# Decoded sequences: values as the left operand in plain fp32, 32 weight columns per pair of heads

## The chip, the cores and the metric

The kernel runs on one core of a Trainium2 chip. The metric is the device time of one execution in microseconds (us); a version is timed in several runs. PE is TensorE (PEld its weight loads), DVE is VectorE, ACT is ScalarE, POOL is GpSimd, and SP is the engine that issues most DMAs.

## What is computed

One layer of a streaming encoder on 512 prompt frames (one sequence) and 8 decoded sequences of 16 frames each (`DEC_BATCH` 8, `DEC_SEQ` 16), that is 640 tokens of width 2048, all in float32. One input projection feeds two groups of heads, whose outputs are normed, joined, projected, and followed by a SwiGLU of width 5632:

```python
def sample_layer(x, ck_a, cv_a, ck_b, cv_b, w_in, norm_mix, rel_table, sinks, ...):
    qa, ka, va, qb, kb, vb = split_proj(rmsnorm(x, norm_mix) @ w_in)
    qb, kb = rope_partial(qb, pos), rope_partial(kb, pos)
    oa = band_attend(qa, concat([ck_a, ka]), concat([cv_a, va]), ..., bias=bias)   # 16 heads of 64
    ob = band_attend(qb, concat([ck_b, kb]), concat([cv_b, vb]), ..., sink=sinks)  # 16 q heads, 2 kv heads
    return merge_and_ffn(x, oa, ob, ...), ka, va, kb, vb

def band_attend(q, k, v, valid, bias=None, sink=None):
    s = einsum('bgqhrd,bgkhd->bghrqk', q, k) * HEAD_DIM ** -0.5        # + bias
    p = exp(s - m)                                                     # m = max (with the sink)
    w = p / (sum(p) + exp(sink - m))                                   # the sink in group B only
    return einsum('bghrqk,bgkhd->bgqhrd', w, v)
```

A decoded sequence of group A has 256 cached keys per head and 16 own ones; one of group B has 128 cached keys and 16 own ones.

## The kernel before

**Split operands.** A matmul operand is mostly held as two fp32r tiles, a rounded part and a rest: `split` writes `hi` on ACT (L179) and `lo = src - hi` on DVE (L180), and `mm3` makes a product of three matmuls (L188 to L190). A matmul whose operands are plain fp32 tiles is given to TensorE as it stands; the transposes (`tr`, L303) and the norms' sums (L232) and spreads (L244) are of that kind. In the trace each of the 42 matmuls of L232 is two records with two weight loads (84 in all); a transpose is one.

**Order of the work.** PE's stream is a row of dense products (`dense`: a chunk of 8 blocks of 128 rows by two halves of 320 tokens by three matmuls; tiles `dn`). After each block `tick` adds `n.rate` to a counter and lets `pump` advance a side job to its next `yield`. Side jobs stand in two queues: `heads` (attention of the prompt, one pair of heads a job) and `decode` (`decode_b`, `decode_a(0)`, then `decode_a(1)`); with two streams they take turns. They come in after four of the eight pairs are projected, with a rate of 1.1. After the last projection `drain_queue("decode")` runs what is left of `decode_a(0)` without ticks between, and advances `heads` jobs in turn with it; then `group_operands` loads the eight tiles of group B's output (`ob_d`), scales and splits them (L183 on ACT, L184 on DVE) and sums their squares (L261 on ACT, L262 on POOL); then comes the output projection of group B (`w_out_b`, 16 blocks `m`), whose ticks pump `decode_a(1)`. At `m == 11` four tiles of `oa_d` are loaded in the same way. The order that the program builds is then changed by a list scheduler, engine by engine, under its own estimates; `keep_pace` holds a side matmul behind the last dense one ahead of it.

**One sequence of `decode_a`.** A job handles a group `g` of 8 heads (four pairs `t` of two heads). For each of the 8 sequences it scatters the 16 queries of each head into zeroed tiles `z` (L633, DVE), loads the cached keys (`cka`), splits them, and makes the scores of all 8 heads at once, 128 rows (8 heads by 16 queries) by 272 keys, in 12 matmuls (4 pairs of 3). Softmax: L656 (bias, maximum), L657, the exponentials with their sums L658 and L659 on ACT, L665 and L666 on DVE (sum, reciprocal). The weights `pt` (unscaled, 128 by 384: 256 cached keys, and 128 columns in which only the sequence's own 16 are not zero) are turned round by `flip`: three transposes and a split. Each half of the cached values (`cva`, 128 keys by 512 columns of 8 heads) is split, and multiplied with the weights as left operand, 512 columns moving: three matmuls per half, and three more with the own values `vh`. The result has 128 rows by 512 columns, of which a head needs its own 64 columns; L684 scales it by `den` (DVE, 128 by 512), four transposes turn it, and two copies (L693) take from it the diagonal blocks.

**One sequence of `decode_b`.** For each of two halves of four sequences it loads keys, values and queries into `S` tiles and splits all of them into pairs of `D` tiles; the own keys are copied from `kb` by POOL. Per sequence: scores in two products of 64 rows by 144 columns (L571), softmax (L574 to L584; here the weights are scaled before they are turned), four transposes, a split, and two products of 256 columns (L592, L593).

**Tiles.** SBUF tiles are drawn from lists (`S`: 128 by 640; `W`: 128 by 1024; `D`: six to ten tiles handed over from other lists); a tile that is drawn again waits for the last use of its former owner.

Of the kernel before, what the change touches and what calls it, by code (L numbers as in the profile page):

```python
# [8 lines left out]
ALU = mybir.AluOpType  # L9
# [265 lines left out]
def diagonal(ap, first):  # L275

    return bass.AP(tensor=ap.tensor, offset=ap.offset + first, ap=[list(ap.ap[0]), [160, 4], [1, DS]])


def r(ap):  # L280
    return ap.bitcast(F32R)


def build(nc, tc, io, pools):
# [32 lines left out]
    sa_d, sb_d = dram("sa_d", (3, P, 8, P)), dram("sb_d", (P, 8, P))  # L317

# [6 lines left out]
    kb = (r(kb0), r(kb1))  # L325
    vb_own = tuple(r(x[:, SP:]) for x in (vb0, vb1))
# [82 lines left out]
    def flip(blocks, lst):  # L409
# [10 lines left out]
        return own, hl  # L420

# [121 lines left out]
    def decode_b():  # L543
        os_b = n.get("W")
        o_s = sh(os_b, 8, P)
        for hf in range(2):
            kraw, vraw, qraw = n.get("S"), n.get("S"), n.get("S")
            dma(out=sh(kraw, 4, CB), in_=io["ckb"][:, 4 * hf:4 * hf + 4])
            dma(out=sh(vraw, 4, P), in_=io["cvb"][:, 4 * hf:4 * hf + 4])
            dma(out=sh(qraw, 8, 64), in_=sb_d[:, :, 64 * hf:64 * hf + 64])  # L550
            yield
            qo, ko, vo = [(n.get("D"), n.get("D")) for _ in range(3)]
            qd = [r(sh(x, 4, 8, DS)) for x in qo]
            n.split(sh(qraw, 8, 64).rearrange("p t (b s) -> p b t s", b=4), *qd)
            kd = [r(sh(x, 4, CB + DS)) for x in ko]
            n.split(sh(kraw, 4, CB), kd[0][:, :, :CB], kd[1][:, :, :CB])
            for e in range(2):
                src = f(kb[e])[:, SP + 64 * hf:SP + 64 * hf + 64].rearrange("p (b s) -> p b s", b=4)
                nc.gpsimd.tensor_copy(kd[e][:, :, CB:], src)
            vd = [r(sh(x, 4, P)) for x in vo]  # L560
            n.split(sh(vraw, 4, P), *vd)
            n.put("S", kraw, vraw, qraw)
            yield
            for bb in range(4):
                b = 4 * hf + bb
                pts = []
                for j in range(2):
                    rows = slice(64 * j, 64 * j + 64)
                    ps = n.bank()[:, :CB + DS]
                    qq = [qd[e][rows, bb].rearrange("p t s -> p (t s)") for e in range(2)]  # L570
                    n.mm3(ps, qq, (kd[0][rows, bb], kd[1][rows, bb]), True, True)  # L571
# [16 lines left out]
                own, pt2 = flip([pts[0][1][:, :P], pts[1][1][:, :P], pts[0][1][:, P:], pts[1][1][:, P:]], "S")  # L588
# [16 lines left out]
    def decode_a(g):  # L605
# [5 lines left out]
        for i in range(3):  # L611
# [6 lines left out]
            else:  # L618
                ps = n.bank().rearrange("p (a b) -> p a b", a=4)
                for j in range(4):  # L620
                    tr(ps[:, j], sv[:, j])
# [5 lines left out]
        for b in range(NB):  # L627
# [60 lines left out]
            for t in range(4):  # L688
                tr(pf[:, P * t:P * t + P], od[:, P * t:P * t + P])
# [527 lines left out]
```

## Time and profile before

| what | us |
|---|---|
| median of 3 runs (lowest, highest) | 2656.42 (2656.01, 2658.73) |
| the profiled execution | 2658.85 |
| its span, first to last instruction | 2657.1 |
| mean granted TensorE clock | 0.992 |

The decoded sequences take part from about 440 us (first scores of `decode_b`: 456 us) to about 830 us (last transpose of the side jobs: 826 us) of the span; the last projection ends at about 664 us, the first product of `w_out_b` begins there. A line of a group gives line, engine, operation, tiles written and read, shape, count, then busy time, mean duration of one in ns, and the engine's idle time ahead of them with what ended it. [...]

### The profile page before, as it was taken

The page shows a single profiled execution, that of the slowest core. Times are in us where ns is not written, and L with a number is a line of the kernel's source. Part 1 is how long each engine was busy: PE and PEld are TensorE (multiplying, and loading weights), DVE is VectorE, ACT ScalarE, POOL GpSimd, SP SyncE. Part 2 cuts the span into 40 slices and gives each one's busy share as a digit, 9 for nine tenths or more (in the row PEclk, how much of TensorE's full clock was granted, in tenths as well). Part 3 has the DMA queues.
Part 4 walks back from the last instruction along what each step waited for, and adds up shares of the span by engine and source line. Part 5 has one row for each costly group of instructions (what it writes and reads, how often), then busy time and mean ns, then how long its engine had stood idle before and what let it go on. Part 6 is the DMA issues. An engine that isn't in the chain of part 4 may idle for free.

```text
span 2657.1 us, 44937 instructions
## 1 busy us (share of the span) xinstructions
PE 2590.4 (97%) x17565; PEld 2532.0 (95%) x17565; DVE 1894.7 (71%) x2934; ACT 1112.5 (42%) x1830; POOL 765.4 (29%) x584
## 2 busy tenths in 40 slices
PE   8999999999999999999999999999999899999996
PEld 8999998999899999999999999999999899999996
DVE  5665566655866877676676677667667988878797
ACT  5443344444633543333333333333334444455553
POOL 0000000000211223433433433343345533444463
PEclk9999999999999999999999999999999899999998
DMA  5322232433655433333333333333335744467665
GB/s 169 106 72 80 90 103 87 129 119 128 221 179 182 155 118 101 118 105 103 123 99 112 119 105 105 114 105 108 119 103 167 222 135 126 134 152 179 154 154 154
DMA packets 162549, 342.58 MB, mean 129 GB/s; under 512 B 19072, under 2 KB 77440, under 8 KB 162336
## 3 DMA queue, kind: packets, MB, share of 16 engines
q1 hardware_dynamic: 151824, 326.92, 38.9%
q0 software_dynamic: 9360, 11.47, 2.7%
q8 instruction: 138, 2.26, 0.4%
q10 hardware_dynamic: 1152, 1.31, 0.1%
q14 instruction: 75, 0.61, 0.1%
HBM read 284.70 MB, written 54.20 MB: 128 GB/s over the span
## 4 chain that ended last, share of the span: by engine, by line
PE 70%; DVE 6%; DMA 3%; issue 2%; ACT 2%; SPq 0%; POOL 0%; DVEq 0%; ACTq 0%; POOLq 0%
PE dn L188 14%; PE dn L190 14%; PE dn L189 14%; PE at L188 9%; PE at L189 9%; PE at L190 9%; DVE W L180 2%; PE at L303 1%; DMA S<-act_d 1%; DVE S L924 1%; DMA W<-w_down 1%; DVE S L180 1%; DMA S<-cka 1%; ACT W L179 1%; DVE S L941 0%
## 5 line engine op out<-in xcount | busy, mean ns | idle before, releaser
L188 PE MATMUL dn<-S,W 128*128 128x320 f32 x3694 | 1161.4, 314 | 11.8 <-DVE S L924 5.5
L190 PE MATMUL dn<-S,W 128*128 128x320 f32 x3694 | 1148.6, 311 | 14.5 <-DVE W L180 14.3
L189 PE MATMUL dn<-S,W 128*128 128x320 f32 x3694 | 1146.6, 310 | 2.0 <-DVE S L180 1.1
L179 ACT ACTIVATE W<-W 128x1024 fp32r<-128x1024 f32 (+2 forms) x632 | 608.2, 963 | 1024.6 <-PE dn L189 538.5
L180 DVE TENSOR_TENSOR W<-W,W 128x1024 fp32r<-128x1024 f32 (+2 forms) x632 | 761.1, 1204 | 157.8 <-ACT W L179 152.6
L188 PEld LDWEIGHTS dn<-S,W 128*128 128x128 f32 x3694 | 697.3, 189 | 24.5 <-issue 9.2
L190 PEld LDWEIGHTS dn<-S,W 128*128 128x128 f32 x3694 | 696.9, 189 | 20.5 <-DVE W L180 19.1
L189 PEld LDWEIGHTS dn<-S,W 128*128 128x128 f32 x3694 | 697.4, 189 | 4.6 <-DVE S L180 1.3
L190 PE MATMUL at<-S,W 128*128 128x320 f32 x1594 | 494.6, 310 | 4.2 <-DVE W L180 4.1
L188 PE MATMUL at<-S,W 128*128 128x320 f32 x1594 | 493.5, 310 | 0.0
L189 PE MATMUL at<-S,W 128*128 128x320 f32 x1594 | 493.3, 309 | 0.0
L907 POOL TENSOR_TENSOR W<-W,W 128x1024 f32<-128x1024 f32 (+2 forms) x76 | 163.4, 2150 | 583.1 <-DVE W L180 502.0
L190 PEld LDWEIGHTS at<-S,W 128*128 128x128 f32 x1594 | 299.8, 188 | 7.7 <-DVE W L180 7.4
L189 PEld LDWEIGHTS at<-S,W 128*128 128x128 f32 x1594 | 300.1, 188 | 0.0
L188 PEld LDWEIGHTS at<-S,W 128*128 128x128 f32 x1594 | 300.0, 188 | 0.0
L924 DVE TENSOR_TENSOR S<-S,dn 128x320 f32<-128x320 f32 x358 | 164.2, 481 | 100.6 <-PE dn L190 99.4
L903 DVE TENSOR_TENSOR W<-W,W 128x1024 f32<-128x1024 f32 (+2 forms) x76 | 135.6, 1784 | 102.9 <-DMA W<-w_up 50.7
L914 POOL TENSOR_TENSOR W<-W,W 128x1024 f32<-128x1024 f32 (+2 forms) x76 | 165.4, 2177 | 105.9 <-DVE W L180 102.8
L924 DVE TENSOR_TENSOR S<-S,at 128x320 f32<-128x320 f32 x262 | 123.3, 480 | 71.2 <-PE at L190 71.2
L262 POOL TENSOR_TENSOR S<-S,S 128x640 f32<-128x640 f32 x40 | 74.6, 1865 | 156.6 <-ACT S L261 153.4
L905 DVE TENSOR_TENSOR W<-W,W 128x1024 f32<-128x1024 f32 (+2 forms) x76 | 82.8, 1090 | 33.4 <-DMA W<-w_gate 25.8
L517 POOL MEMSET S<- 80x640 f32 x9 | 6.3, 695 | 330.0 <-DMA ob_d<-S 212.2
(153 smaller groups left out, 2269.2 us busy)
## 6 DMA issues: line engine op xcount, KB each, us to landing
W<-w_gate SPq DMA_DIRECT2D x88, 512.0 KB
W<-w_up SPq DMA_DIRECT2D x88, 512.0 KB
W<-w_in SPq DMA_DIRECT2D x66, 512.0 KB
W<-w_down SPq DMA_DIRECT2D x64, 384.0 KB
W<-w_down SPq DMA_DIRECT2D x68, 320.0 KB
act_d<-S SPq DMA_DIRECT2D x63, 320.0 KB
half<-act_d SPq DMA_DIRECT2D x81, 160.0 KB
S<-act_d SPq DMA_DIRECT2D x80, 160.0 KB
```

The costliest lines, as they stand in the source:

```text
L179: self.nc.scalar.activation(hi, src, AF.Identity)
L180: self.nc.vector.tensor_tensor(lo, src, f(hi), ALU.subtract)
L188: mm(out, a[0], b[0], start=first, stop=False)
L189: mm(out, a[0], b[1], start=False, stop=False)
L190: mm(out, a[1], b[0], start=False, stop=last)
L262: (eng or nc.gpsimd).tensor_tensor(ssq, ssq, sq, ALU.add)
L303: nc.tensor.transpose(out, src, n.ident)
L903: nc.vector.tensor_tensor(b12[:, w], b12[:, w], b22[:, w], sub)
L905: nc.vector.tensor_tensor(s6[:, w], b11[:, w], b12[:, w], sub)
L907: nc.gpsimd.tensor_tensor(b11[:, w], b22[:, w], s6[:, w], sub)
L914: nc.gpsimd.tensor_tensor(b21[:, w], b21[:, w], s6[:, w], sub)
L924: add = lambda o, a, b: nc.vector.tensor_tensor(o, a, b, ALU.add)
```

## The change

Group A's weights are now scaled in place by `den` (one DVE operation of 128 by 384, ahead of the turn), turned by three transposes and copied once by ACT as plain fp32 (`flip_whole`). Cached values stay as they were loaded, and the own ones are copied once as plain fp32 (`v_own`). The product is turned round: for each pair `t` the 128 value columns of its two heads are the left operand and 32 columns of weights (two heads by 16 queries) move, for two cached halves and the own block: 12 plain fp32 matmuls, which give the output in the layout that is needed; L684, the four transposes and the strided `diagonal` are gone. A sequence of `decode_a` has 10 `yield`s now, and had 14. In group B queries, keys, values and weights are plain fp32: one matmul per product in place of three; the own keys and values take a way through a DRAM tile `kv_d`, and all loads go straight into `D` tiles.

```diff
+    def flip_whole(blocks, lst):
+        w = P * len(blocks)
+        ps = n.bank()[:, :w]
+        for i, src in enumerate(blocks):
+            tr(ps[:, P * i:P * i + P], src)
+        own = n.get(lst)
+        nc.scalar.activation(own[:, :w], ps, AF.Identity)
+        return own
...
     def decode_b():
...
-            kraw, vraw, qraw = n.get("S"), n.get("S"), n.get("S")
-            dma(out=sh(kraw, 4, CB), in_=io["ckb"][:, 4 * hf:4 * hf + 4])
...
+            ko, vo, qraw, qo = (n.get("D") for _ in range(4))
+            kd, vd, qd = sh(ko, 4, CB + DS), sh(vo, 4, P), sh(qo, 4, P)
+            dma(out=kd[:, :, :CB], in_=io["ckb"][:, 4 * hf:4 * hf + 4])
+            dma(out=kd[:, :, CB:], in_=kv_d[0, :, 64 * hf:64 * hf + 64].rearrange("p (b s) -> p b s", b=4))
...
-                    n.mm3(ps, qq, (kd[0][rows, bb], kd[1][rows, bb]), True, True)
+                    nc.tensor.matmul(ps, qd[rows, bb], kd[rows, bb], start=True, stop=True)
...
-                n.mm3(po, (vd[0][:, bb], vd[1][:, bb]), cut(pt2, 0, 256), True, False)
-                n.mm3(po, vb_own, cut(pt2, 256, 512), False, True)
+                nc.tensor.matmul(po, vd[:, bb], own[:, :256], start=True, stop=False)
+                nc.tensor.matmul(po, v_own[:, :P], own[:, 256:512], start=False, stop=True)
...
     def decode_a(g):
...
             nc.vector.reciprocal(den, den)
+            nc.vector.tensor_scalar(pt[:, :CA + P], pt[:, :CA + P], den, None, ALU.mult)
             yield
             yield
-            own3, p3 = flip([pt[:, P * j:P * j + P] for j in range(3)], "S")
+            own3 = flip_whole([pt[:, P * j:P * j + P] for j in range(3)], "S")
             n.put("S", pt)
             yield
+            yield
             po = n.bank()
-            for j in range(2):
-                two, vd = pair("S", 512)
-                n.split(raws[j][:, :512], *vd)
-                n.put("S", raws[j])
-                yield
-                yield
-                n.mm3(po, cut(p3, P * j, P * j + P), vd, j == 0, False)
-                n.put("S", *two)
-            n.mm3(po, cut(p3, 256, 384), [x.rearrange("p a b -> p (a b)") for x in vh], False, True)
-            n.put("S", *own3)
-            od = n.get("S")
-            nc.vector.tensor_scalar(od[:, :512], po, den, None, ALU.mult)
-            yield
-            yield
-            pf = n.bank()
+            keys = (*raws, v_own)
             for t in range(4):
-                tr(pf[:, P * t:P * t + P], od[:, P * t:P * t + P])
-            n.put("S", od)
+                for j, v in enumerate(keys):
+                    nc.tensor.matmul(po[:, 32 * t:32 * t + 32], v[:, P * t:P * t + P],
+                                     own3[:, P * j + 32 * t:P * j + 32 * t + 32],
+                                     start=t == j == 0, stop=(t, j) == (3, 2))
+            n.put("S", own3, *raws)
...
-                nc.vector.tensor_copy(sh(o_s, 4, P)[rows, :, own], diagonal(pf[rows], DS * rr))
+                nc.vector.tensor_copy(sh(o_s, 4, P)[rows, :, own],
+                                      sh(po, 4, 32)[rows, :, DS * rr:DS * rr + DS])
+            yield
```

In the rows below, a name is a tile with its number of the build; `dn` are dense products, `at` the banks of the side jobs, and lines move down by up to 9 in the changed file (transposes L303 become L298, scores of the prompt L379 become L374). Rows follow each other on the engine.

PE, in `w_out_b`, from the turn of a sequence's weights (`decode_a(1)`, its third sequence here) to the product with the values, before:

```order
L303 MATMUL at_8244<-cst,S_1466_8207 128x128 x3
L190 MATMUL dn_8231<-S_1364_7775,W_1474_8234 128x320
L188 MATMUL dn_8231<-S_1368_7784,W_1473_8233 128x320
L189 MATMUL dn_8231<-S_1369_7785,W_1473_8233 128x320
L190 MATMUL dn_8231<-S_1368_7784,W_1474_8234 128x320
L188 MATMUL dn_8231<-S_1368_7784,W_1473_8233 128x320
L189 MATMUL dn_8231<-S_1369_7785,W_1473_8233 128x320
L190 MATMUL dn_8231<-S_1368_7784,W_1474_8234 128x320
L188 MATMUL at_8258<-S_1479_8259,S_1476_8248 128x512
```

and after (the second sequence):

```order
L298 MATMUL at_8106<-cst,S_1397_8087 128x128 x3
L188 MATMUL dn_8033<-S_1273_7489,W_1389_8035 128x320
L189 MATMUL dn_8033<-S_1274_7490,W_1389_8035 128x320
L190 MATMUL dn_8033<-S_1273_7489,W_1390_8036 128x320
L188 MATMUL dn_8033<-S_1273_7489,W_1389_8035 128x320
L675 MATMUL at_8124<-S_1401_8110,S_1398_8093 128x32
L675 MATMUL at_8124<-S_1401_8110,S_1399_8094 128x32
L675 MATMUL at_8124<-S_1401_8110,S_1309_7602 128x32
```

Between the turn and the product stand four dense matmuls now. This is so in 7 of the 16 sequences; in 3 more there are six or eight, in the others 19 rows and more. Between the last scores and the turn there stand at least 18 dense matmuls or other side work as long; before, 11 or 12 in half of the sequences.

DVE, one sequence of `decode_a(1)` from its maximum (L656, then L653) to the copies of its output, before:

```order
L656 ISA S_1501_8394,sm_8391<-at_8329,S_1398_7860 128x272
L656 ISA sm_8391 128x1
L633 CAST S_1400_7862<-S_1403_7868 64x4x16 x2
L657 TENSOR_SCALAR sm_8391<-sm_8391 128x1
L180 TENSOR_TENSOR S_1548_8636<-S_1534_8571,S_1547_8635 128x512
L665 TENSOR_TENSOR sm_8392<-sm_8392,sm_8393 128x1
L666 RECIPROCAL sm_8392<-sm_8392 128x1
L180 TENSOR_TENSOR S_1507_8418<-at_8413,S_1506_8417 128x384
L797 TENSOR_TENSOR S_1514_8452<-dn_8342,S_1358_7764 128x640
```

and after:

```order
L653 ISA S_1419_8224,sm_8221<-at_8159,S_1289_7533 128x272
L653 ISA sm_8221 128x1
L630 CAST S_1291_7535<-S_1294_7541 64x4x16 x2
L654 TENSOR_SCALAR sm_8221<-sm_8221 128x1
L662 TENSOR_TENSOR sm_8222<-sm_8222,sm_8223 128x1
L663 RECIPROCAL sm_8222<-sm_8222 128x1
L664 TENSOR_SCALAR S_1420_8225<-S_1420_8225,sm_8222 128x384
L681 COPY S_1288_7532<-at_8262 64x4x16 x2
```

The turn now comes after L662, L663 and L664, ahead of which it stood before; the splits of the values and of the turned weights (L180) and the scaling of the result (L684, further down) are gone.

PE, at the end of the last projection (`dn_7302` before, `dn_7274` after are its bank; `dn_7840` and `dn_7509` are the first of `w_out_b`), before:

```order
L190 MATMUL dn_7302<-S_72_213,W_1272_7415 128x320
L188 MATMUL dn_7840<-S_1361_7768,W_1395_7842 128x320
L303 MATMUL at_7526<-cst,S_1290_7521 128x128 x4
L188 MATMUL at_7491<-S_1288_7511,S_1283_7481 128x512
L189 MATMUL at_7491<-S_1289_7512,S_1283_7481 128x512
```

and after:

```order
L190 MATMUL dn_7274<-S_72_214,W_1242_7366 128x320
L188 MATMUL dn_7509<-S_1250_7437,W_1284_7511 128x320
L189 MATMUL dn_7509<-S_1251_7438,W_1284_7511 128x320
L190 MATMUL dn_7509<-S_1250_7437,W_1285_7512 128x320
L188 MATMUL dn_7509<-S_1250_7437,W_1284_7511 128x320
L189 MATMUL dn_7509<-S_1251_7438,W_1284_7511 128x320
```

Before, `decode_a(0)` still had its sequences 6 (in part) and 7 to do at this point, and the attention of the last pair of prompt heads ran between too. With fewer `yield`s `decode_a(0)` ends within the last projection, 84 dense matmuls ahead of its end: `w_out_b` runs on in a row, and the last pair of heads is pumped within it, in turn with `decode_a(1)`.

More of the change, by code (lines that the diff above doesn't have):

```diff
@@ L708, in build @@
     dma(out=io["o_kb"], in_=kf)
-    n.split(kf, *kb)
+    n.split(kf[:, :SP], *kb)
+    dma(out=kv_d[0], in_=kf[:, SP:])
     n.put("F", kf)
@@ L715, in build @@
     tr(ps, vf[:, SP:])
-    n.split(ps, *vb_own)
+    vs = n.scratch()[:, :P]
+    nc.scalar.activation(vs, ps, AF.Identity)
+    dma(out=kv_d[1], in_=vs)
     n.put("F", vf)
```

55 lines of the change are left out of this document (22 added, 33 removed).

## The prediction

> **What bounds the kernel now.** First the page: engine totals and the chain that ended last.
>
> ```profile
> span 2657.1 us, 44937 instructions
> PE 2590.4 (97%) x17565; PEld 2532.0 (95%) x17565; DVE 1894.7 (71%) x2934; ACT 1112.5 (42%) x1830; POOL 765.4 (29%) x584
> PE 70%; DVE 6%; DMA 3%; issue 2%; ACT 2%; SPq 0%; POOL 0%; DVEq 0%; ACTq 0%; POOLq 0%
> ```
>
> PE is busy for 97% of the span and makes 70% of the chain. DVE and ACT time alone is worth nothing; the change counts by what PE has to do and by how long PE waits. Second, the stretches with decoded work (columns: length, then busy us of PE, PEld, DVE, ACT and POOL with counts, clock, DMA share, GB/s), and one of the FFN beside them:
>
> ```profile
> 440.00:655.00 215.00, 211.65 (x1433) 197.04 (x1433) 135.55 (x356) 93.54 (x211) 12.97 (x53) 1.00 0.39 122
> 655.00:705.00 50.00, 46.54 (x305) 40.85 (x304) 41.95 (x103) 36.85 (x78) 15.95 (x21) 1.00 0.63 201
> 705.00:830.00 125.00, 120.35 (x781) 114.39 (x780) 79.83 (x159) 42.47 (x81) 14.53 (x32) 0.99 0.58 190
> 440.00:840.00 400.00, 388.55 (x2582) 362.27 (x2582) 265.79 (x623) 180.38 (x377) 48.73 (x109) 1.00 0.48 157
> 1000.00:2045.00 1045.00, 1045.00 (x7129) 1045.00 (x7129) 723.32 (x767) 365.54 (x396) 397.57 (x217) 1.00 0.34 111
> ```
>
> From 440 to 840 us PE is idle for 400 - 388.55 = 11.45 us. That is the size of what fewer waits can bring there, beside some 0.16 us more at each wait (a 320 column matmul lasts 0.31 us but the next starts after 0.147), which the busy column hides. DVE is busy for 66% and ACT for 45%: neither is the bound.
>
> **Prices on PE**, from start to start. The timeline of PE around a value product of group A, around four transposes, and around six plain fp32 matmuls (12 records):
>
> ```profile
> 648.25 0.39 PE L188 MATMUL at<-S,S 128*128 128x512 f32 x1
> ...
> 649.64 0.30 PE L188 MATMUL dn<-S,W 128*128 128x320 f32 x1
> 110.24 0.60 PE L303 MATMUL at<-cst,S 128*128 128x128 f32 x4
> 110.59 0.39 PE L188 MATMUL dn<-S,W 128*128 128x320 f32 x1
> 110.83 0.31 PE L189 MATMUL dn<-S,W 128*128 128x320 f32 x1
> 696.20 1.39 PE L232 MATMUL at<-cst,S 128*128 128x1 f32 x12
> 697.45 0.39 PE L188 MATMUL dn<-S,W 128*128 128x320 f32 x1
> 697.68 0.31 PE L189 MATMUL dn<-S,W 128*128 128x320 f32 x1
> ```
>
> Six matmuls of 512 columns: 1.39 us, 0.231 each. Four transposes: 110.83 - 110.24 less one dense matmul (0.147) = 0.44, 0.110 each. Twelve fp32 records with one column: 697.68 - 696.20 - 0.147 = 1.33, 0.111 each. With one column to move, that is the loading of 128 columns of weights; a plain fp32 matmul is two such records, 0.222 us.
>
> **Group A on PE.** Per sequence and job, 16 times: nine matmuls of 512 columns (9 x 0.231 = 2.08) and four transposes (0.44) go; twelve fp32 matmuls come, 24 records x 0.111 = 2.66, since 32 columns are nearer to L232's one than to anything that fills the load. So +0.14 each, **+2.3 us**. A way past the load isn't to be seen: every record has other weights.
>
> **Group B on PE.** Per sequence:
>
> ```profile
> 456.04 0.31 PE L190 MATMUL dn<-S,W 128*128 128x320 f32 x1
> 456.27 0.34 PE L188 MATMUL at<-S,S 64*128 64x144 f32 x2
> ...
> 457.02 0.31 PE L189 MATMUL dn<-S,W 128*128 128x320 f32 x1
> 484.68 0.28 PE L188 MATMUL at<-S,S 128*128 128x256 f32 x1
> ...
> 485.40 0.31 PE L188 MATMUL dn<-S,W 128*128 128x320 f32 x1
> ```
>
> The scores: six matmuls take 457.02 - 456.04 - 2 x 0.147 = 0.69. Four fp32 records come. If each streams as an fp32r one does, the load sets 0.111 each (0.44); if each needs two steps a column, 288 steps, which is next to a dense matmul of 320 (0.147; 0.13 by proportion) gives 0.53. The values: six of 256 columns take 0.72; four records come, at 0.12 each (0.48) by the first reading, or at the 0.231 of 512 columns (0.92) by the second. No row has a plain fp32 matmul with more than 128 columns, so both ends stand: -0.25 to -0.16 and -0.24 to +0.20, times 8. I take the slow end, -1.3 and +1.6, **+0.3 us**, since two records for one matmul say that the operands are cut up, and keep -3.9 as the other end.
>
> [...] The 84 records of 42 matmuls speak for two loads.
>
> **Waits on the turned weights (group A).** Groups of PE's transposes and of the operations at issue, and the timeline of one turn:
>
> ```profile
> L303 PE MATMUL at<-cst,S 128*128 128x128 f32 x461 | 76.4, 278 | 10.0 <-ACT S L658 5.8 <-DVE S L583 1.6 <-DVE S L684 1.2
> L407 DVE TENSOR_SCALAR S<-S,sm 128x384 f32<-128x384 f32 x16 | 6.6, 414 | 0.0
> L684 DVE TENSOR_SCALAR S<-at,sm 128x512 f32<-128x512 f32 x16 | 11.9, 746 | 7.9 <-PE at L190 7.1 <-POOL S L645 0.7
> 657.86 0.29 PE L190 MATMUL at<-S,S 128*128 128x272 f32 x1
> 659.46 0.51 ACT L658 ACTIVATE S<-S,sm 128x256 f32<-128x256 f32 x1 [3.91 <-DVE sm L657]
> 660.12 0.62 PE L303 MATMUL at<-cst,S 128*128 128x128 f32 x3 [0.35 <-ACT S L658]
> 660.58 0.16 DVE L666 RECIPROCAL sm<-sm 128x1 f32<-128x1 f32 x1
> 660.77 0.49 ACT L179 ACTIVATE S<-at 128x384 fp32r<-128x384 f32 x1 [0.42 <-PE at L303]
> ```
>
> The turn waits 5.8 us in all for the exponentials, in 8 places, 7.1 with the hidden 0.16 each. Now it starts 2.26 us after the last score matmul (657.86 to 660.12). With the scaling ahead of it, it can start at 660.74 + 0.41 and a hand-over, some 661.2: 3.3 us. The order gives 18 to 20 dense matmuls as cover in 6 places (18.5 x 0.147 = 2.7, with the mode's 0.1 some 2.85), so 0.45 us each, 2.7; in the others the cover is longer. A DVE split of 0.69 that happens to stand ahead in half of them adds about 3. So 5.7 in place of 7.1, **-1.4 us** (from -7, all covered, to +7, a delay at each of 16).
>
> The four transposes that waited for L684 (1.2 us on PE, three waits, 1.7 with the hidden part) go: **-1.7**.
>
> **A new wait: the product on ACT's copy.** In the rows above the copied weights are ready at 661.26, 1.14 us after the first transpose started. In 7 places the product stands behind three transposes and four dense matmuls, 0.33 + 0.59 + 0.1 = 1.0: 0.15 us each, 1.1 in all, and where a weight split (1.06 us on ACT) stands ahead of the copy, up to that more. I take one such, **+2**; from 0 to 10 x 1.06. Behind the waiting matmul stands all dense work, so it is paid in full.
>
> **The end of the projections.** Before, 40 us of side work with hardly any dense matmuls lie there, and the loading of group B's output beside it. PE's waits:
>
> ```profile
> 664.56 0.41 PE L188 MATMUL dn<-S,W 128*128 128x320 f32 x1 [0.34 <-ACT S L183]
> 679.24 0.42 PE L189 MATMUL dn<-S,W 128*128 128x320 f32 x1 [0.96 <-DVE S L184]
> 691.66 0.39 PE L196 MATMUL at<-S,W 128*128 128x256 f32 x1 [0.61 <-DVE S L180]
> 692.52 0.41 PE L303 MATMUL at<-cst,S 128*128 128x128 f32 x2 [0.32 <-DMA S<-sa_d]
> L183 ACT ACTIVATE S<-S,cst 128x640 fp32r<-128x640 f32 x8 | 6.6, 824 | 3.4 <-DMA S<-ob_d 3.4
> L261 ACT ACTIVATE S<-S 128x640 f32<-128x640 f32 x7 | 5.1, 731 | 0.0
> ```
>
> The stretch 655 to 705 has 50 - 46.54 = 3.46 us idle, 4.4 with six hidden parts. After, the eight tiles can be made beside 84 dense matmuls (12.3 us): ACT needs 8 x (0.82 + 0.73) = 12.4, and the first tile is ahead of them. So nearly all of it goes: **-4** (from 0, if tiles in slots that the projection still reads come late, to -6).
>
> **At no cost.** DVE loses per sequence two value splits, the turned weights' split and L684 and gains the scaling, about 2.3 us, 36 in all; ACT two splits of the values. PE's dense work was ready anyway (FFN row: PE never idle at a DVE share of 69%). SP gets five DMAs more (`kv_d`), issued under projections; a late one would cost PE a DMA's landing, as here:
>
> ```profile
> 687.95 4.43 DMA S<-sa_d
> ```
>
> The second half's queries now go into a tile that the first half's last product reads; until its scores there are 36 matmuls, some 5 us, against 4.4 and ACT's copy. I book 0, at worst +1.
>
> **Sum.** +2.3 + 0.3 - 1.4 - 1.7 + 2 - 4 = -2.5 us. The profiled execution, 2658.85, would come to 2656.4; the median of the runs shown is 2.4 below it, so the forecast is **2654 us** (2656.42 - 2.5), within the 0.2% (5.3 us) that a measurement of this kernel can tell from no change.
>
> **Rivals.**
> - Faster. The relief of DVE and ACT takes three quarters of the 11.45 us of idle time (8.6), and group B streams at the fast end (-3.9 with A's +2.3): 2656.4 - 8.6 - 1.6 = 2646. For it: nearly all waits are on DVE or ACT. Against: the longest chain, scores to turn, gets longer. Chance 0.27.
> - Slower: the copy on ACT. If a weight split stands ahead of it at the ten places with up to eight dense matmuls between, PE loses 10 x 1.06 = 10.6; with +2.6 of PE work and -4: 2666. It decides from some 0.8 us a place. For it: ACT takes its work in order, and some copies stand right behind such a split. Against: ACT is 45% busy. Chance 0.13.
> - [...] Chance 0.02.
> - The forecast, waits of another kind for the same time: 0.58.
>
> **Range.** 2646 to 2664: from the faster rival to just under the slower. Faster by over 0.2%: 0.27; within: 0.58; slower: 0.15.
>
> **What the profile after should show.** L675: 384 records (16 x 24) with 0.111 us from start to start; group B's product at 0.12 or 0.23. No idle time of PE on L183 or L184 ahead of `w_out_b`, and its bank following the projection's at once. L298 waiting for DVE L664 rather than for ACT, some 6 us in all; L675 waiting for L423, 1 to 3 us. PE's idle time from 440 to 840 near 8 us. I am wrong if L675 waits for over 0.5 us at a place, if its records take more than 0.12, or if the load of values (`cva`) becomes what L675 waits for: before, ACT's splits waited for it.

## The result, and the profile after

The changed kernel takes 2678.93 us (median of 4 runs, 2674.09 to 2681.80) against 2656.22 (4 runs, 2655.69 to 2658.73): slower, ratio 1.0082, 95% interval 1.0063 to 1.0100. The profiled execution has a span of 2674.7 us, 17.6 more than before.

The page's engine totals, and the stretches that were read before (length, busy us of PE, PEld, DVE, ACT and POOL with counts, granted clock, DMA share, GB/s):

```profile
span 2674.7 us, 45112 instructions
PE 2605.4 (97%) x17709; PEld 2553.8 (95%) x17709; DVE 1847.0 (69%) x2869; ACT 1092.0 (41%) x1794; POOL 769.4 (29%) x580
440.00:655.00 215.00, 209.17 (x1416) 195.18 (x1415) 113.03 (x329) 80.98 (x193) 15.85 (x51) 0.97 0.37 115
655.00:705.00 50.00, 46.21 (x322) 43.69 (x321) 35.50 (x66) 29.03 (x54) 17.87 (x18) 0.97 0.61 197
705.00:830.00 125.00, 118.75 (x795) 115.53 (x794) 66.20 (x153) 40.43 (x84) 15.00 (x34) 0.92 0.56 179
440.00:840.00 400.00, 384.13 (x2602) 364.40 (x2601) 218.69 (x552) 152.96 (x333) 48.72 (x102) 0.95 0.46 146
```

DVE and ACT have less to do, as forecast, and PE 144 records more (17709 against 17565). What the sum had not at all is the third column from the right: the granted clock, 1.00 from 440 to 840 us before, is 0.95 now and 0.92 from 705 to 830. PE's idle time is 15.87 us there (400 - 384.13), 4.4 more than before.

The trace's clock is at one of two values, full and half (1.00 and 0.50). In the decoded part it is at half in five stretches now (37.5 us in all) and was in one before (3.4 us, at 800.6). Around one of them, timeline rows of all engines, and the stretches ahead of it, in it and in the longest one:

```profile
735.31 0.31 PE L190 MATMUL dn<-S,W 128*128 128x320 f32 x1
736.05 0.42 DVE L664 TENSOR_SCALAR S<-S,sm 128x384 f32<-128x384 f32 x1
736.62 0.52 PE L298 MATMUL at<-cst,S 128*128 128x128 f32 x3 [1.00 <-DVE S L664]
737.17 0.49 ACT L423 ACTIVATE S<-at 128x384 f32<-128x384 f32 x1 [1.62 <-PE at L298]
737.42 0.30 PE L188 MATMUL dn<-S,W 128*128 128x320 f32 x1
...
740.21 1.47 PE L675 MATMUL at<-S,S 128*128 128x32 f32 x6
741.49 0.61 PE L189 MATMUL dn<-S,W 128*128 128x320 f32 x1
741.90 0.47 PE L190 MATMUL dn<-S,W 128*128 128x320 f32 x1
742.17 0.47 PE L188 MATMUL dn<-S,W 128*128 128x320 f32 x1
742.43 0.47 PE L189 MATMUL dn<-S,W 128*128 128x320 f32 x1
```

```profile
735.85:739.26 3.41, 2.64 (x21) 2.42 (x21) 0.51 (x2) 0.49 (x1) 0.00 (x0) 1.00 0.92 325
739.26:746.08 6.82, 6.82 (x29) 6.82 (x29) 2.48 (x5) 2.10 (x3) 0.75 (x3) 0.50 0.35 130
810.94:824.59 13.65, 13.18 (x57) 13.21 (x58) 4.74 (x8) 2.28 (x3) 1.66 (x2) 0.50 0.17 48
```

The transposes wait 1.0 us for the scaling, four dense matmuls follow, then the product with the values. At 739.26 the clock falls. Dense matmuls then start 0.267 us apart (741.90, 742.17, 742.43) in place of 0.147, records of the product 0.213 (741.49 - 740.21 over 6) in place of 0.11. In a stretch at half clock some 45% of the time is lost: 37.5 x 0.46 = 17 us, 1.5 before. The first row of the stretches is the surprise: in the 3.41 us ahead of the fall PE was listed as busy for 2.64.

The edges of the clock in this trace lie on one grid of 3.41 us (from 739.26 to 810.94 there are 21 steps). For each step of the grid I counted how long columns were streaming. It is an estimate: columns of each matmul by 0.42 ns, twice for plain fp32, since records of L589 and L590 with 256 columns start 0.215 us apart, 0.84 ns a column, where fp32r matmuls with 512 start 0.231 apart, 0.45 ns a column. The steps ahead of the five falls, and the lowest steps at full clock that were followed by none:

```
fall at us          531.0  599.3  684.6  739.3  810.9
half clock for us     6.8    6.8    3.4    6.8   13.7
share streamed ahead 0.30   0.38   0.33   0.36   0.23
longest wait ahead   2.8    1.3    4.1    1.3    3.1   (start to start of PE)

no fall, step at    636.9  715.4  551.5  752.9  677.8
share streamed       0.37   0.38   0.39   0.39   0.43
```

By this count the threshold lies near 0.37 to 0.38, and the same count parts the steps of all 20 traces of this study. From 440 to 2600 us, 96 steps at full clock were followed by a fall, all with shares of up to 0.38; 12432 were not, all with shares of 0.365 and more. (Transposes count as plain fp32. The prompt's scores, fp32r on 64 of the 128 rows, count half each: those with 256 columns start in pairs, at 484.34 and 484.35 for one.) How busy PE is listed does not part them: 79 of the steps without a fall have PE busy for 0.6 of the time or less, and five falls, in `a_only` and `narrow_defer_sq` below, follow a step in which PE was busy throughout. Here is one such step of each kernel, first of a_only, then of narrow_defer_sq, where L674 is the product, and PE's rows in the latter:

```profile
794.91:798.32 3.41, 3.41 (x29) 3.41 (x30) 0.44 (x2) 0.00 (x0) 0.00 (x0) 1.00 0.83 317
806.25:809.66 3.41, 3.41 (x29) 3.27 (x29) 0.36 (x2) 0.09 (x1) 0.00 (x0) 1.00 0.38 118
806.09 0.30 PE L189 MATMUL dn<-S,W 128*128 128x320 f32 x1
806.39 2.87 PE L674 MATMUL at<-S,S 128*128 128x32 f32 x24
809.09 0.39 PE L190 MATMUL dn<-S,W 128*128 128x320 f32 x1
```

A product of 24 records with 32 columns streams 24 x 64 x 0.42 = 0.65 us of its 2.66, 0.24; with 0.75 us of dense matmuls to fill the step without a gap, that is 0.39. So the product by itself stands at the threshold. A wait of a microsecond in the same step brought it below (1.00 us at 736.62, share 0.36); in the rows above, 0.15 us did, by which the product started late (806.39 - 806.09 - 0.147; share 0.32).

PE's waits from 440 to 840 us (total, times, longest):

```profile
PE at L298 <- DVE S L664: 8.1, 10, 2.8
PE at L298 <- DVE S L363: 4.5, 2, 3.8
PE at L298 <- ACT W L179: 2.5, 1, 2.5
PE at L675 <- ACT S L423: 0.4, 1, 0.4
```

Each run comes with its mean clock, so its time can be cut in two: what the clock took (span x (1 - clock), an upper bound, since idle time at half clock costs nothing) and the rest. The clock is given to 0.001, which is 2.7 us. Both parts are means over a kernel's runs, so they do not add up to the median exactly. All kernels of this study; each ratio is to the runs of before on the same chip, and the row of before has those of one chip (the runs of before on other chips give 16.6 to 18.6 and 2636.3 to 2638.3):

| kernel | median us | ratio to before (95%) | clock us | rest us |
|---|---|---|---|---|
| before (20 runs) | 2654.9 | | 18.3 | 2636.7 |
| after | 2678.9 | 1.0082 (1.0063 to 1.0100) | 36.1 | 2642.3 |
| a_only | 2681.7 | 1.0100 (1.0086 to 1.0114) | 36.8 | 2644.6 |
| b_only | 2653.4 | 0.9994 (0.9986 to 1.0003) | 19.8 | 2634.1 |
| w64 | 2668.2 | 1.0053 (1.0040 to 1.0066) | 29.3 | 2639.7 |
| wide | 2665.9 | 1.0043 (1.0029 to 1.0058) | 24.0 | 2642.1 |
| spread | 2665.4 | 1.0036 (1.0022 to 1.0050) | 24.5 | 2640.0 |
| late_turn | 2670.1 | 1.0061 (1.0048 to 1.0073) | 32.6 | 2638.5 |
| wide_late | 2664.0 | 1.0033 (1.0021 to 1.0044) | 24.4 | 2639.3 |
| before10 | 2660.6 | 1.0021 (1.0012 to 1.0030) | 22.7 | 2638.0 |
| wide14 | 2666.5 | 1.0042 (1.0029 to 1.0055) | 24.5 | 2641.7 |
| b18 | 2676.4 | 1.0081 (1.0068 to 1.0095) | 30.1 | 2646.5 |
| warm | 2661.6 | 1.0027 (1.0016 to 1.0039) | 18.0 | 2643.9 |
| b_warm | 2658.3 | 1.0012 (1.0003 to 1.0020) | 17.6 | 2640.6 |
| noscale | 2656.4 | 1.0005 (0.9996 to 1.0014) | 20.3 | 2636.2 |
| wide_sq | 2657.8 | 1.0009 (1.0000 to 1.0018) | 19.8 | 2638.2 |
| b_sq | 2659.3 | 1.0014 (1.0005 to 1.0024) | 22.2 | 2636.4 |
| defer | 2660.0 | 1.0022 (1.0013 to 1.0031) | 21.8 | 2638.8 |
| defer_sq | 2656.9 | 1.0007 (0.9998 to 1.0015) | 18.6 | 2638.4 |
| narrow_defer_sq | 2656.7 | 1.0011 (1.0002 to 1.0020) | 22.9 | 2634.7 |

Of the change's loss, some 17.8 us are the clock (36.1 - 18.3) and 5.6 the rest.

### The profile page after: what moved, and what is told of

The parts are those of the page before. It is cut to its first block, busy times and chain, and to the rows that moved or that the text cites. A ratio compares the mean times of both kernels' runs of the same rounds, so it can differ in the third digit from the quotient of the medians.

```text
span 2674.7 us, 45112 instructions
## 1 busy us (share of the span) xinstructions
PE 2605.4 (97%) x17709; PEld 2553.8 (95%) x17709; DVE 1847.0 (69%) x2869; ACT 1092.0 (41%) x1794; POOL 769.4 (29%) x580
## 4 chain that ended last, share of the span: by engine, by line
PE 85%; DVE 7%; DMA 3%; ACT 2%; issue 2%; SPq 0%; POOL 0%; DVEq 0%; ACTq 0%; POOLq 0%
PE dn L188 18%; PE dn L190 18%; PE dn L189 18%; PE at L190 8%; PE at L188 8%; PE at L189 8%; DVE W L180 2%; PE at L675 2%; PE at L298 2%; PE at L374 1%; DMA S<-act_d 1%; DVE S L917 1%; DMA W<-w_down 1%; ACT W L179 1%; PE at L196 1%
## 5 line engine op out<-in xcount | busy, mean ns | idle before, releaser
L180 DVE TENSOR_TENSOR W<-W,W 128x1024 fp32r<-128x1024 f32 (+2 forms) x632 | 758.3, 1200 | 160.9 <-ACT W L179 155.6
L190 PEld LDWEIGHTS dn<-S,W 128*128 128x128 f32 x3694 | 699.6, 189 | 20.0 <-DVE W L180 18.6
L262 POOL TENSOR_TENSOR S<-S,S 128x640 f32<-128x640 f32 x40 | 77.4, 1936 | 173.9 <-ACT S L261 173.1
L898 DVE TENSOR_TENSOR W<-W,W 128x1024 f32<-128x1024 f32 (+2 forms) x76 | 82.1, 1080 | 29.6 <-DMA W<-w_gate 24.4
```

What stands on the lines that cost most here:

```text
L180: self.nc.vector.tensor_tensor(lo, src, f(hi), ALU.subtract)
L190: mm(out, a[1], b[0], start=False, stop=last)
L262: (eng or nc.gpsimd).tensor_tensor(ssq, ssq, sq, ALU.add)
L898: nc.vector.tensor_tensor(s6[:, w], b11[:, w], b12[:, w], sub)
```

## The experiments

**Is it the clock, and what brings it down?** The width of the product came first. `wide` is after with this edit:

```diff
-                    nc.tensor.matmul(po[:, 32 * t:32 * t + 32], v[:, P * t:P * t + P],
-                                     own3[:, P * j + 32 * t:P * j + 32 * t + 32],
+                    nc.tensor.matmul(po[:, P * t:P * t + P], v[:, P * t:P * t + P],
+                                     own3[:, P * j:P * j + P],
...
-                                      sh(po, 4, 32)[rows, :, DS * rr:DS * rr + DS])
+                                      diagonal(po[rows], DS * rr))
```

> All 128 columns of the turned weights move through each value block in place of 32; same number of matmuls, same order on PE, and the copies take the diagonal. In the changed kernel the granted clock is 0.95 from 440 to 840 us (five stretches at half clock, 37.6 us) against 1.00 before. Theory 1, the clock falls after a stretch of 3.4 us in which few columns stream, however long the matmuls are listed as busy: 128 columns fill the time that the loading of weights takes, so L675 stays at 0.111 us from start to start, stretches at half clock remain only behind waits of some 2.8 us and more (three), 10 to 14 us in all, and the time falls by 10 to 14 us, to 2665 to 2669. Theory 2, the waits of the transposes for L664 bring the clock down and the shape of the product has no part in it: same as the changed kernel, 2676 to 2682. Theory 3, a plain fp32 record is paid by its columns: L675 rises to 0.21 us and the time to 2700 or more.

2665.9 us, 13.0 below after; the clock's part falls from 36.1 to 24.0, the rest stays (2642.3 and 2642.1). Four times the columns take no longer: the trace of wide has the product and its neighbours so, and the stretches and waits:

```profile
745.31 0.30 PE L188 MATMUL dn<-S,W 128*128 128x320 f32 x1
745.61 2.94 PE L675 MATMUL at<-S,S 128*128 128x128 f32 x24
748.31 0.39 PE L189 MATMUL dn<-S,W 128*128 128x320 f32 x1
```

```profile
440.00:655.00 215.00, 210.06 (x1464) 195.91 (x1463) 116.05 (x339) 83.77 (x200) 17.02 (x53) 1.00 0.38 120
705.00:840.00 135.00, 129.16 (x929) 125.46 (x928) 75.08 (x152) 45.24 (x84) 22.15 (x38) 1.00 0.61 195
440.00:840.00 400.00, 385.05 (x2709) 365.13 (x2708) 229.16 (x563) 160.13 (x341) 56.00 (x107) 1.00 0.49 156
```

```profile
PE at L298 <- DVE S L664: 7.7, 10, 2.3
PE at L298 <- DVE S L363: 4.9, 2, 4.2
```

24 records in 2.70 us (748.31 - 745.61), 0.112 each, as with 32 columns. The waits are the same as after's, and the clock stays up but for one stretch behind the wait of 4.2 us. So the waits alone don't bring it down, and theory 2 falls; nor are columns the price (theory 3).

`w64` moves 64 columns (two pairs of heads, of which the copies take one):

> 64 columns move in place of 32 (two pairs of heads, of which one is kept); order and matmuls as in the changed kernel. Theory 1, a threshold on the streamed share: the product's own share is 0.48 in place of 0.24, stretches with a wait of about 1 us come to 0.45 to 0.55, above the threshold, so the clock is as with 128 columns: 2664 to 2670. Rival, the loss goes down with the columns in proportion: half way between 32 and 128 columns, some 2672 to 2674.

2668.2, inside theory 1's band, though not for its reason. It had the clock as with 128 columns, but the clock's part, 29.3, lies between those of 32 and 128: in the profiled execution it falls three times from 440 to 840 (676, 731, 806 us; shares of 0.17, 0.37 and 0.38 ahead), so 64 columns still leave two steps at the threshold.

`spread` puts `if t: yield` ahead of each pair's three matmuls:

> One more yield between the pairs of heads, so that the 24 records of a product fall into four pieces of six with dense matmuls between. Theory 1 (few streamed columns in 3.4 us): each stretch of 3.4 us holds some 0.7 to 1.4 us of the product at most, so half clock only behind the long waits, 10 to 14 us in all: 2663 to 2670. Thirteen yields in place of ten also move the end of group A's first half later, up to 4 us the other way. Theory 2 (the waits alone): same as the changed kernel, 2676 to 2682, clock near 0.95 from 440 to 840.

2665.4. The same cure by another way: the records are as narrow as after's, but stand in pieces of six between dense matmuls, and the clock's part is wide's (24.5 and 24.0).

`late_turn` moves the last `yield` of a sequence to behind L664, and `wide_late` does so in wide:

> The changed kernel with one of group A's ten yields moved from the end of a sequence to between the scaling L664 and the transposes, so that the transposes wait less; 32 columns as in the changed kernel. Theory 1 (half clock after 3.4 us in which columns stream for less than some 0.37 of the time): the product alone with the dense matmuls around it gives 0.38 to 0.39, so with short waits it stays above, and half clock is left only behind the two or three waits of 2.8 us and more: 2663 to 2670, clock from 440 to 840 near 0.98 to 0.99. Rival, the 32 columns bring the clock down whatever the transposes wait for: 2674 to 2682.

> 128 columns and the moved yield together. From wide's 2666: of its 7.7 us of waits for L664 some 5 go, and what remains above the kernel before is group A's price on PE (2.3 us) and the waits at the end of the projections: 2658 to 2663. If the waits come back in another place, or the moved yield makes other work late: 2664 to 2668.

2670.1 and 2664.0. In late_turn nine steps with the narrow product stay at full clock with shares of 0.38 to 0.41; the clock falls only behind three waits of about 3 us. That is 8.8 us less than after, 3.5 of them the clock's part, just above theory 1's band (the clock from 440 to 840 us is 0.97, below what it said); with the same yields 128 columns are 6 us better still. Wide_late lies 1 us above its first band: the waits for L664 hardly fell (7.5 us in 8 places), and the one in front of the transposes of the prompt stayed (5.1).

**Which half of the change?** Before with group A's change alone, and after with group A as before:

> The kernel before with group A's change alone; group B as before. Theory 1: the loss is group A's, so 2670 to 2680 and several stretches at half clock in the decoded part. Rival, group B's unsplit operands are to blame (their loads straight into D tiles, the fp32 product): within 3 us of 2656.

> The changed kernel with group A as before; group B's change alone. Theory 1: within 3 us of 2656 with the clock as before (scores at 0.11 us a record, values at 0.215, together some 0.5 us less on PE than before in eight sequences). Rival (group B is to blame): 2668 to 2680.

2681.7 (1.7 above its band) and 2653.4. The loss is group A's. Group B's change has no measurable effect (ratio 0.9994, 0.9986 to 1.0003). Its prices are read from these rows of after:

```profile
441.70 0.31 PE L190 MATMUL dn<-S,W 128*128 128x320 f32 x1
441.94 0.52 PE L567 MATMUL at<-S,S 64*128 64x144 f32 x4
442.38 0.41 PE L188 MATMUL dn<-S,W 128*128 128x320 f32 x1
442.63 0.31 PE L189 MATMUL dn<-S,W 128*128 128x320 f32 x1
...
448.00 0.59 PE L589 MATMUL at<-S,S 128*128 128x256 f32 x2
448.43 0.59 PE L590 MATMUL at<-S,S 128*128 128x256 f32 x2
448.68 0.50 PE L188 MATMUL dn<-S,W 128*128 128x320 f32 x1
449.02 0.30 PE L189 MATMUL dn<-S,W 128*128 128x320 f32 x1
```

Measured as the 0.69 of before was, from the dense matmul ahead to the second one behind, the scores take 442.63 - 441.70 - 2 x 0.147 = 0.64. The values take 449.02 - 0.147 - 448.00 = 0.87, against 0.72. That is -0.05 and +0.15, +0.8 us for eight sequences. The 0.5 us less of b_only's expectation came from taking 0.11 for each score record, against a 0.69 that holds more than the records: 0.08 us of it pass before the first of them starts (456.27 - 456.04 - 0.147).

**The pace.** `before10` takes four `yield`s out of before's `decode_a` (one of the two behind each half's split, both ahead of the turn of the output):

> The kernel before with ten yields a sequence of group A in place of fourteen: the pace of the changed kernel, nothing else of it. The prediction's term for the end of the projections (group A's first half ends within the last projection, group_operands lies beside dense matmuls): 2652 to 2654. Rival, the wait there moves from L183 and L184 to a transpose of the prompt that stands behind them on DVE, as in the changed kernel (one wait of 3.8 us for L363), and shorter cover in group A adds waits: 2656 to 2662.

2660.6: ten yields alone cost 6 us. The rival held: the wait at the end of the projections is now one of 4.6 us, behind which the clock falls for 6.8 us.

```profile
PE at L303 <- ACT S L658: 5.4, 7, 3.2
PE at L303 <- DVE S L368: 4.6, 1, 4.6
```

More yields do not give it back. `wide14` is wide with four more (three between the pairs, one behind L664); `b18` is b_only with eighteen in `decode_a`:

> 128 columns, and fourteen yields a sequence of group A as in the kernel before (three between the pairs of heads, one between the scaling and the transposes). If the pace of ten yields costs as much here as alone (6 us: 2660.6 against 2654.5): wide_late's 2664 becomes 2657 to 2660, of which 2.3 us are group A's price on PE. Rival, the pace is costless here, since the loss of the kernel with ten yields was its own splits and scaling with shorter cover: 2662 to 2666.

> Group B's change alone, and eighteen yields a sequence of group A in place of fourteen. If more cover goes on helping as from ten to fourteen (6 us): 2648 to 2651. If at fourteen the covers are long enough, or group A's first half now ends so late that more side work has no dense matmuls beside it: 2653 to 2658.

2666.5 and 2676.4, the first at the end of its rival's band, the second far outside what I expected. In wide14 the transposes wait more for L664, for a reason that these runs don't show. In b18 group A's first half runs further past the end of the last projection than in before (its last scores start at 691 us, and at 674 there), and from 655 to 705 us PE is busy for 42.6 of 50 us at a clock of 0.84:

```profile
PE at L298 <- DVE S L664: 13.2, 12, 4.4
```

```profile
655.00:705.00 50.00, 42.62 (x221) 35.13 (x221) 44.13 (x99) 31.35 (x70) 18.84 (x23) 0.84 0.51 166
```

**What else holds wide 11 us above before?** `noscale` is wide without L664; `wide_sq` is wide with `add_square(..., nc.vector)` in `group_operands`; `b_sq` is b_only with the same:

> wide without L664: the weights are turned unscaled, so the output of group A lacks the division by the sums. If the scaling chain is what holds the transposes: the waits for L664 (7.7 us in ten places) become waits for the exponentials of some 3 us, and the time goes from 2666 to 2659 to 2662. If the waits are set by what the turn is queued behind (weight splits on ACT and DVE): 2664 to 2667.

> wide with the sums of squares in group_operands on DVE in place of POOL. If POOL's additions (L262, 1.93 us) are what stretches L184 from 0.88 to 1.6 us beside them, L184 falls to 0.9, and DVE with the 0.82 us more for each addition is as long as before: the wait for L363 at the end of the projections (4 to 5 us) falls by 0 to 2 us; 2663 to 2667. If the additions on DVE lie in its path: 2667 to 2672.

> Group B's change alone, with the sums of squares in group_operands on DVE. Faster L184 (waits of 1.0 for L184 and 0.3 us for L183 go): 2650 to 2653, below both kernels. DVE's additions in the path: 2654 to 2660.

Noscale: 2656.4, 9.5 below wide and 3 below the band. Its transposes wait for the exponentials, and half as long:

```profile
PE at L298 <- DVE S L363: 5.1, 2, 3.9
PE at L298 <- ACT S L655: 3.7, 7, 1.8
```

Wide_sq: 2657.8, 8.1 below wide and 5 below its band, more than the wait alone. Groups of L184 and of the additions from 640 to 700 us, of wide and then of wide_sq:

```profile
L262 POOL TENSOR_TENSOR S<-S,S 128x640 f32<-128x640 f32 x7 | 13.5, 1930 | 14.7 <-ACT S L261 14.3
L184 DVE SCALAR_TENSOR_TENSOR S<-S,cst,S 128x640 fp32r<-128x640 f32 x8 | 12.6, 1599 | 2.9 <-DMA oa_d<-S 1.5 <-ACT S L183 1.4
```

```profile
L184 DVE SCALAR_TENSOR_TENSOR S<-S,cst,S 128x640 fp32r<-128x640 f32 x8 | 7.1, 882 | 2.3 <-ACT S L183 1.3 <-DMA oa_d<-S 1.0
L262 DVE TENSOR_TENSOR S<-S,S 128x640 f32<-128x640 f32 x7 | 5.7, 819 | 0.1
```

L184 takes 0.88 us without additions on POOL beside it and 1.60 on average where they run there; both together on DVE take 12.8 us in place of 12.6. The longest wait for L363 falls from 4.2 to 1.7 us and the clock no longer falls behind it. In b_sq L184 falls too (1.22 to 0.92), but the kernel is 6 us slower than b_only: the order of the side work was moved with it, and a spread of a norm (L244) now waits 3.2 us for DVE, a transpose 2.4 us for a DMA. So a gain of one edit of this kind need not carry over to a neighbouring kernel.

Noscale leaves the division out, so it is no version to use. `defer` is noscale with the division done: the reciprocals of a group's eight sequences are spread over the rows of `o_s` by four plain fp32 products at the end of the group, and multiplied there once. `defer_sq` has wide_sq's edit too, `narrow_defer_sq` moves 32 columns again:

```diff
-            nc.vector.reciprocal(den, den)
-            nc.vector.tensor_scalar(pt[:, :CA + P], pt[:, :CA + P], den, None, ALU.mult)
+            nc.vector.reciprocal(bias[:, 304 + b:305 + b], den)
...
+        for t in range(4):
+            nc.tensor.matmul(ps[:, P * t:P * t + P], sel[:, P * t:P * t + P], sel[:, 512:], start=True, stop=True)
+        nc.vector.tensor_tensor(o_s[:, :512], o_s[:, :512], ps, ALU.mult)
```

> The same with the squares on POOL as before: noscale (2656.4) with the division done at the group's end: 2656 to 2660. If the chain at the end of a group (products, multiplication, store, then the loading of oa_d) holds group_operands up: 2660 to 2664.

> wide_sq, and L664 is replaced: the reciprocals of a group's eight sequences are kept, spread by four plain fp32 products over the rows of the output at the group's end (0.9 us of PE a group) and multiplied there once (DVE). If the two gains add (9.5 and 8.1) less some 2 us for the spreading: 2649 to 2653, below both kernels. If the order of the side work, moved again, gives back one of them: 2654 to 2660.

> defer_sq with 32 columns moving. If the narrow product alone stays at a streamed share of 0.38 to 0.39 and falls below the threshold only beside a wait: with few waits left 1 to 5 us above defer_sq. If 32 columns bring the clock down by themselves: 8 to 13 us above defer_sq.

2660.0, 2656.9 and 2656.7. The two gains don't add: defer_sq is no better than wide_sq or noscale alone. The last one matters most: with the same narrow product as in the change, but with most of the waits beside it gone, the time is that of 128 columns, below both of its bands. Its reason held in part only. The clock's part is 4.3 us larger (22.9 against 18.6), with three falls against one from 440 to 840, and all three follow a step in which PE was busy throughout: three of the sixteen products bring the clock down without a listed wait in the step. The rest is 3.7 smaller; why it is smaller stays open. From 440 to 840, defer_sq and then narrow_defer_sq:

```profile
440.00:840.00 400.00, 391.49 (x2769) 373.35 (x2768) 227.53 (x575) 160.72 (x343) 27.33 (x93) 1.00 0.49 159
```

```profile
440.00:840.00 400.00, 393.38 (x2761) 375.53 (x2760) 226.91 (x574) 160.38 (x342) 30.24 (x93) 0.99 0.49 159
```

**Filling waits elsewhere.** `warm` is before, `b_warm` b_only, each with products of constants on PE ahead of the FFN's first product and of its second half:

```diff
+    def fill(k):
+        at, ps = n.emitted(), n.bank()
+        for _ in range(k):
+            nc.tensor.matmul(ps[:, :256], cst[:, :P], cst[:, :256], start=True, stop=True)
+        n.side.append((at, n.emitted()))
...
+    fill(4)     # ahead of the first pair of w_gate and w_up
...
+    fill(9)     # ahead of the first step of w_down
```

> The kernel before, and plain fp32 products of constants that nothing reads, on PE alone: 4 ahead of the FFN's first product (1.7 us in a wait of 1.95) and 9 ahead of the second half's first (3.8 us in a wait of 5.1). Theory 1: the stretches of 3.4 us there no longer fall below a streamed share of 0.37, so the half clock at 968 us (3.4 us) and most of that at 2060 us (13.7 us) go, and some 40 to 60 dense matmuls start 0.147 in place of 0.267 us apart: faster by 3 to 6 us, 2649 to 2652. Rival, the clock doesn't follow what streams: no gain, or up to 1 us slower.

> Group B's change alone, with the same products of constants. Both gains together: 2646 to 2650, which would be below both kernels. If the filling has no use: 2652 to 2655 as group B's change alone.

2661.6 and 2658.3: slower than the kernels without the fill by 7 and 5, outside all bands. The fill stood in the place it was meant for, but the waits moved behind it instead of being filled: in warm the 18 records end at 2061.4, and a wait of 3.7 us for DVE L924 comes two microseconds later, with the clock falling there as before (the clock's part is 18.0 against 18.3). That tells nothing against theory 1, and nothing for it. The 7 us lie behind the second fill. That it takes one of four banks may be why; no run here shows it.

No version lies below both kernels by more than the measurement can tell; b_only, at 0.9994, comes nearest.

## Why the prediction was wrong

Forecast 2654, range 2646 to 2664, "within 0.2%"; measured 2678.9. The step that failed is the one under "Prices on PE" and "Group A on PE": a record was taken to cost its 0.111 us and nothing more. The price itself held at full clock (24 records in 2.6 to 2.7 us, with 32 as with 128 columns). What the sum lacked is that such a product, whose records start 0.11 us apart with 32 columns as with 128, streams for only 0.24 of its time, so that the clock fell to half in or behind it (at 739.26, for one, with a share of 0.36 ahead), however busy PE was listed. The clock took up to some 17.8 us of the loss. Wide took back 13.0 us by the width alone, and spread as much by the place. No rival had it. A second step failed beside it: the two terms that made waits shorter, -1.4 on the turned weights and -4 at the end of the projections, came out as longer waits.

The other terms, one by one:

- Waits on the turned weights, "5.7 in place of 7.1": 8.1 us are listed (7.7 at full clock in wide), against 5.8 listed before. The estimate of 0.45 us a place was near where covers are short (0.45 to 1.0), but the chain also ran behind other work on DVE, with waits of up to 2.8. In that longest one, two additions of POOL (L262) ran from 807.25 to 811.04 us; beside them an L184 ahead of L664 took 2.11 us, and L664 itself 1.68 in place of 0.42. Taking the scaling out gave 9.5 us, more than the waits it removed; the order of the side work moved too, and what that gave is not shown by itself.
- The transposes that waited for L684, -1.7: gone, as forecast (the trace lists one such wait before, of 1.2 us, not three).
- The copy on ACT, +2: held. One wait of 0.4 us is listed, but in eight of the sixteen sequences L675 starts 0.05 us after the copy's end, seven times 0.15 us later than a dense matmul would have followed and once 0.6, some 1.7 in all. The slower rival (2666 through that copy) had the right sign and the wrong cause.
- The end of the projections, -4: of the wrong sign. The wait for L183 and L184 did go, but the transposes of the prompt then stood behind three L184 of 2.1 us each on DVE, 3.8 us, and the clock fell after it. The term counted ACT's work beside the dense matmuls (12.4 us) and not DVE's, which lasts longer beside POOL's additions (L184 2.1 us in place of 0.88). Before10 has the pace alone, with shorter covers in group A beside it: +6 in place of -4.
- Group B, +0.3: +0.8 by its records. The slow end that the sum took held for both: from the first record the scores take 0.54 (442.63 - 441.94 - 0.147) where 0.53 was forecast, the values 0.87 where it was 0.92. What was wrong is the -0.16 to -0.25 for the scores: it set the records alone against 0.69, which holds more than the records. B_only measured -1.6 us, with an uncertainty that reaches from -3.7 to +0.8.
- Two records a plain fp32 matmul, 0.111 us each: held at full clock (L675 has 384 records for 192 matmuls), so more than two weight loads for each are excluded.
- DVE's and ACT's relief at no gain: held. DVE has 47 us less to do from 440 to 840, and PE waits longer.

The sum of the rest comes out near: +2.3 for group A, +4.4 of idle time from 440 to 840, +0.8 for group B give 7.5 against a measured 5.6 (4.0 to 6.0 with the runs of before on other chips). Of what the profile after was to show, L675's 384 records, its short waits for L423 and the end of the waits for L183 and L184 came true; PE's idle time is 15.9 us in place of near 8. Of the three signs named for a wrong forecast one is there, in the stretches at half clock: L675's records take more than 0.12 (0.213). The values come in time, and L675's longest listed wait is 0.4 us. Two things should have been seen: the clock's part of the time before was 21 us (1 - 0.992 of the span) and was never asked for its cause, and the trace of before has a fall at 800.6 us behind a wait of 2.8. One figure of the section on the profile before is to be corrected: the first scores of `decode_b` are at 413 us, not at 456, so the stretch from 440 holds five of its eight sequences.

## What to carry to other kernels

Ask of each stretch of a matmul program not only how long PE is listed as busy, but how long columns stream in it. Here a block of plain fp32 matmuls that each load 128 columns of weights to move 32 streamed for 0.24 of its time. With a wait of a microsecond beside it, and three times in narrow_defer_sq without one, it halved the clock for at least 3.41 us, some 1.6 us lost each time. Widening the moving side cost nothing here up to 128 columns (0.112 us a record); interleaving with dense matmuls did as well; taking most of the waits away left 10.2 us at half clock from 440 to 840 in narrow_defer_sq, in place of 37.5. Where a change takes work from engines that aren't the bound, look at what it puts in the chain that the bound waits for: here leaving out one operation of 0.42 us ahead of the transposes (noscale) took back 9.5 us, while the splits that went gained nothing that a run shows.

## What the runs showed of the hardware

- The clock: half, in multiples of 3.41 us, after a step with a share of streamed columns, counted as above, below some 0.37 to 0.38, however busy PE is listed (from 440 to 2600 us, 96 falls in 20 traces, 12432 steps without one). Back to full after steps with 0.78 and more (a column counted twice as long at half clock); after steps with up to 0.76 it stayed at half.
- At half clock L675's records with 32 columns start 0.213 us apart in place of 0.111, dense matmuls 0.267 in place of 0.147.
- A plain fp32 matmul is two records in the trace (a transpose one). With 256 columns they start 0.215 us apart, where an fp32r matmul takes 0.12 for 256 and 0.231 for 512. With 1, 32 and 128 columns they start 0.111 to 0.112 us apart, as the weight loads of those with 1 and 32 do: up to 128 the columns set no price.
- On 64 rows, four plain records with 144 columns took 0.44 us together from the first start to the next dense one, in two pairs: the two of a pair start 0.01 us apart, the pairs 0.22, so two records ran at a time.
- DVE beside POOL: L184 (128x640) took 0.88 us with no addition of POOL beside it and up to 2.2 beside them, L664 (128x384) 0.42 and 1.68.
